# A decoder block on one core: weight sums with two transfers and two additions a unit, loaded one at a time, and the last unit's values added by VectorE

## The chip, the core and the metric

The kernel runs on one core of one Trainium2 chip. The metric is the device time of one execution in microseconds. The core has five instruction streams that matter here: TensorE (PE, matrix products into the PSUM banks), VectorE (DVE), ScalarE (ACT), GpSimd (POOL) and SyncE (SP). SyncE issues most transfers between the chip's memory (HBM) and the on-chip buffer (SBUF); GpSimd issues the transfers that add what they bring to what already lies at the destination (`accum_op=ALU.add`, called accumulating transfers below).

## What is computed

One decoder block over 16 meta tokens and 512 tokens of width 1024, in float32:

```python
h = layer_norm(concat([meta, x]), emb_ln_g, emb_ln_b)
proj = h @ w_in                                # 1024 x 10240, split in ten parts of 1024 columns
q_d, k_d, v_d, g_d, q_s, k_s, v_s, g_s, m_d, m_s = split(proj)
y_d = rms_norm(differential_attention(q_d, k_d, v_d)) * (1 - lam_init)   # 8 heads, softmax with ALiBi
y_s = stick_breaking_attention(q_s, k_s, v_s)                            # 16 heads of 64
br_d = (y_d * silu(g_d)) @ w_br_diff
br_s = (y_s * silu(g_s)) @ w_br_sb
merged = sigmoid(m_d + b_gate[0]) * br_d + sigmoid(m_s + b_gate[1]) * br_s
h = layer_norm(2 ** 0.25 * h + merged @ w_out, ln_g, ln_b)
return h[16:]
```

Every product of float32 values is made of three TensorE products of rounded parts: high x high, high x low and low x high.

## The kernel before

**Units.** The work is cut into 16 units (`UNITS`, line 70): eight differential heads ("d"), then eight pairs of stick-breaking heads ("s"). In unit u TensorE computes the scores and values of unit u, and among them, as filling, the key and value projections of unit u+1, the query projection of unit u+2 and some gates. `run` (line 571) takes the projections as generators and calls the other steps when an estimated time has come. After the units come the branch products ("BD", "BS"), the merge and the output product.

**Weights.** `items` (line 89) lists all operands in the order in which the products use them, each 128 x 512; `loads` lists what SyncE must bring for them. `prep(h)` (line 192) is called once a product and prepares the operand four products ahead: `hi` casts it on ScalarE into the rounded high part `wh` (line 183), `lo` subtracts on VectorE to get the low part `wl` (line 188), `add` makes a sum where the next operand is one, and `fetch` issues loads for which a buffer has come free. `wh` and `wl` have six buffers each. The loads have rings of their own: `raw` (six buffers) for plain tiles, `rawk` (five) for the sums of the key and value weights, `rawa` (four) for those of the branch weights.

**Seven products in place of eight.** From unit 5 on (`SEVEN`) the keys and values of a unit are computed together, with one 2 x 2 block scheme that needs seven products and sums of weight blocks (`stage_kv`, line 674, its products on line 693). With a11, a12 (halves of the key weights) and a21, a22 (halves of the value weights) the operands are, in this order: a11, a21+a11, a21+a22+a11, a12, a21+a22, a22, and a21+a22+a11+a12. Three `rawk` tiles a unit hold sums: a21 is loaded by SyncE, and GpSimd then issues one or two accumulating transfers on top (four a unit). The seventh operand is an addition on VectorE (line 169). The branch products use the same seven operands, but there the third is also an addition on VectorE, into a tile `sum`, so that two accumulating transfers do.

**When the sums are loaded.** `fetch` (line 134) goes through two lists, the `rawk` loads first, and issues as many as there are buffers free. `rawk` has no pool until unit 1 (line 958). A tile's accumulating transfers are written into the program three and six calls of `prep` after its load, through `placed` (line 222), which ties an instruction behind the one that stands ahead of it on its engine.

**What sets the order.** Ahead of the units and behind them the order of each engine is tied as written (`keep_order`). In the units only what goes through `placed` or `behind` is; the rest is ordered by the framework's scheduler, which may let an instruction go before others of its engine that are not ready yet. Each engine runs its instructions in the order that comes out.

**Keys.** The projected keys are cast into a staging tile `ks`, and SyncE copies them into the tiles `K[0]` and `K[1]` (lines 646 and 647), of which there is one set: the copy for unit u+1 waits for the scores of unit u (line 759), and the scores of unit u+1 wait for the copy.

**Biases.** GpSimd makes the slopes of each differential head by scaling the last head's tile (line 827, two buffers), at the start of each unit in program order.

**Values of the stick-breaking units.** `s_values` (line 918) gets each head's result in two halves of the 128 partitions. ScalarE copies one half across into `half` (line 933) and the other into `ys` (line 934), and GpSimd issues an accumulating transfer that adds `half` to `ys` (line 935). The gate (line 528) multiplies the result. In the last unit `ys` is a row of `ysT`, and behind its gate come the first splits for the branch products (`operands`, line 1030).

Of the kernel before, what the change touches and what calls it, by code (L numbers as in the profile page):

```python
# [9 lines left out]
F32 = mybir.dt.float32  # L10
# [3 lines left out]
ALU = mybir.AluOpType  # L14
PSUM = bass.MemoryType.PSUM

P = 128
# [18 lines left out]
ORDERED = [mybir.EngineType.PE, mybir.EngineType.DVE, mybir.EngineType.Activation, mybir.EngineType.Pool]  # L36
WARM = 14
SEVEN = 5
# [7 lines left out]
def hybrid_block_kernel(ctx: ExitStack, tc: tile.TileContext, x, meta, emb_g, emb_b, w_in, b_gate,  # L46
                        diff_lambda, subln_g, w_br_d, w_br_s, w_out, ln_g, ln_b, out):
    nc = tc.nc
    v, s, g, pe = nc.vector, nc.scalar, nc.gpsimd, nc.tensor
# [39 lines left out]
    items, names, loads = [], [], []  # L89
    for n, (kind, i) in enumerate(seq):  # L90
        if kind in ("BD", "BS", "wd", "ws"):
            if kind[0] == "B":
                tiles = [(w_br_d if kind == "BD" else w_br_s)[:, :, ts(2 * i + m, P)] for m in range(2)]
            else:
                tiles = [w_in[:, :, ds(COL[x + kind[1]] + i * P, P)] for x in "kv"]
            (a11, a12), (a21, a22) = [[w[:, ts(k, 4)] for k in range(2)] for w in tiles]
            ring = "rawa" if kind[0] == "B" else "rawk"
            o = len(loads)
            if ring == "rawa":
                loads += [(a11, None, "raw"), (a21, (a11,), ring), (a21, (a22,), ring), (a12, None, "raw"), (a22, None, "raw")]  # L100
                items += [o, o + 1, (o + 2, o), o + 3, o + 2, o + 4, (None, o + 3)]
            else:
                loads += [(a11, None, "raw"), (a21, (a11,), ring), (a21, (a22, a11), ring), (a12, None, "raw"),
                          (a21, (a22,), ring), (a22, None, "raw")]
                items += [o, o + 1, o + 2, o + 3, o + 4, o + 5, (o + 2, o + 3)]
        elif n < 4:
            items += [None, None]
        else:
            c = COL[kind] + i * P
            items += [len(loads), len(loads) + 1]  # L110
            loads += [(w_in[:, ts(k, 4), c:c + P], None, "raw") for k in range(2)]
        names += [(kind, i)] * (len(items) - len(names))
# [9 lines left out]
        left[l] = 1  # L122
    raw0 = ypool.tile([P, 4, KT, P], F32, tag="ys", name="raw0")
    raws, second, split, sums, later = {}, {}, [], {}, []
    rings = {"raw": (6, []), "rawk": (5, []), "rawa": (4, [])}
    sum_loads, other_loads = [[l for l, x in enumerate(loads) if (x[2] == "rawk") == y] for y in (True, False)]
    state = {"h": 0, "n": 0, "ahead": 4}
    pools = {"raw": wpool}
# [4 lines left out]

    def fetch(most=99):

        for order in (sum_loads, other_loads):
            while order and most:
                l = order[0]
                src, more, tag = loads[l]
                bufs, log = rings[tag]  # L140
                if len(log) >= bufs and left[log[-bufs]] or tag not in pools:
                    break
                raw = pools[tag].tile([P, 4, P], F32, tag=tag, name=tag, bufs=bufs)
                nc.sync.dma_start(raw if l < WOUT else raw.rearrange("p a b -> p (a b)"), src)
                if more is not None:
                    second[l] = [lambda raw=raw, x=x: g.dma_start(raw, x, accum_op=ALU.add) for x in more]  # L146
                    if tag == "rawa":
                        added(l)
                    else:
                        for n in range(len(more)):  # L150
                            later.append((state["n"] + 3 + 3 * n, lambda l=l: added(l)))
                        later.sort(key=lambda x: x[0])
                raws[l] = raw
                log.append(order.pop(0))
                most -= 1

    def added(l):

        if second.get(l):
            placed(second[l].pop(0), ORDERED[3:])  # L160

    def add(h):

        first, other = items[h]
        one = sums.pop(True) if first is None else raws[first]
        raw = one
        if first is not None and loads[first][2] == "rawa":
            raw = lp.tile([P, 4, P], F32, tag="sum", name="sum", bufs=1)
        v.tensor_tensor(raw, one, raws[other], op=ALU.add)
        for l in items[h]:  # L170
            if l is not None:
                left[l] -= 1
        sums[h] = sums[True] = raw

    def hi(h):

        assert len(split) == h
        item = items[h]
        assert not second.get(item)
        raw = raw0[:, h // 2, ts(h % 2, 4)] if item is None else sums.pop(h) if isinstance(item, tuple) else raws[item]  # L180
        wh, wl = [wpool.tile([P, 4, P], F32R, tag=w, name=w, bufs=6) for w in ("wh", "wl")]
        split.append((raw, wh, wl))
        s.copy(wh, raw)  # L183
# [38 lines left out]
    def placed(work, engines=ORDERED):  # L222

        ins = nc.cur_bb.bb.instructions
        n = len(ins)
        work()
        for e in engines:
            new = next((i for i in ins[n:] if i.engine == e), None)
            old = next((ins[m] for m in range(n - 1, max(n - 400, 0), -1) if ins[m].engine == e), None)
            if new is not None and old is not None:  # L230
                follow(new, old)
# [349 lines left out]


    with tc.tile_pool(name="att", bufs=1) as ap:
        apads = []
        for n in range(2):
            a = ap.tile([P, AW], F32, name=f"apad{n}")
# [331 lines left out]
        def s_values(unit, c, p, ta):  # L918
            V = unit["V"]
            v4, a4 = tails[c]  # L920
            own, oth = ((LO, HI), (HI, LO))[c]
            av = pav.tile([P, 512], F32, tag="av", name="av")
            pe.matmul(av, V[c][:, 0, :], ta[0][0], start=True, stop=False)
            pe.matmul(av[:, QOFF[4]:], v4, a4, start=False, stop=False)
            for j in range(1, 4):
                o = av[:, QOFF[j]:]
                pe.matmul(o, V[c][:, j, :], ta[j][0], start=False, stop=False)  # L927
                pe.matmul(o, V[c][:, j, :], ta[j][1], start=False, stop=False)
            pe.matmul(av, V[c][:, 0, :], ta[0][1], start=False, stop=True)
            if "y" not in unit:  # L930
                unit["y"] = gpool.tile([P, S], F32, tag="sg", name="ys")
            half = ap.tile([P, S], F32, tag="sq", name="half")
            s.copy(half[own], av[oth])
            s.copy(unit["y"][own], av[own])
            placed(lambda: g.dma_start(unit["y"][own], half[own], accum_op=ALU.add), ORDERED[3:])

# [18 lines left out]
        pending = []  # L955
        for u, (kind, n) in enumerate(UNITS):
            unit = units[u]
            if u + 4 == SEVEN:
                pools["rawk"] = ap
            last = u + 1 == len(UNITS)  # L960
            proj = [] if last else keys_values(units[u + 1], *UNITS[u + 1])
# [62 lines left out]
    first = len(nc.cur_bb.bb.instructions)  # L1024
    lp = ctx.enter_context(tc.tile_pool(name="late", bufs=1))
    lr = ctx.enter_context(tc.tile_pool(name="later", bufs=2))
    pools["rawa"] = lp
    LEFT, RIGHT = ts(0, 256), ts(1, 256)

    def operands(y):  # L1030
# [225 lines left out]
```

## Time and profile before

| what | before |
|---|---|
| median of three runs | 729.81 us (729.35 to 733.26) |
| profiled execution | 724.71 us |
| its span, first to last instruction | 722.9 us |
| granted TensorE clock | 0.996 |
| GpSimd's accumulating transfers for `rawk` | 44 of 256 KB, 6.0 us to landing |
| SyncE's loads for `rawk` | 33 of 256 KB, 4.1 us to landing |
| moved by DMA in all | 123.64 MB |

The profile is one execution. A row of the page's first part gives an engine's busy time, its share of the span and its instructions. A row of the table of stretches gives the stretch, its length, and then for PE, PEld (weight loads), DVE, ACT and POOL the busy time and the number of instructions, then the granted TensorE clock, the DMA share (mean busy share of 16 DMA engines; it can pass 1 where a transfer is counted whole) and GB/s. A row of the waits reads "who waited <- for whom: us in total, times, longest". A row of a timeline gives start, duration, engine (with "q" for an issue by an engine's sequencer), line, operation, output<-inputs, shape, count, and in brackets the idle time before it with what ended it. Times of TensorE's instructions overlap: a matmul's end is modelled, so the spacing of starts tells its rate.

### The profile page before, as it was taken

Reading aid. Unit: us, or ns where it says so; the run is one execution under the profiler, and the core shown is the slowest. Engines: PE = TensorE matmul, PEld = TensorE weight load, DVE = VectorE, ACT = ScalarE, POOL = GpSimd, SP = SyncE. Lnnn points to the kernel's source line nnn. Section 1 sums busy time; section 2 is a strip of 40 time slices with the busy share of each in tenths; the row PEclk is TensorE's granted clock in tenths of the full one; section 3 lists DMA queues with packets and bytes.
Section 4 is the critical chain, followed back from the end, with each engine's and each line's share of the span. In section 5 each row is a group of like instructions: output and inputs, shape, how many; then the busy total and the mean of one; then the engine's idle time right before and its main releaser. Section 6 shows DMA issues by size and latency. Waiting matters only on the chain.

```text
span 722.9 us, 13508 instructions
## 1 busy us (share of the span) xinstructions
PE 706.7 (98%) x4558; PEld 644.5 (89%) x4558; DVE 571.3 (79%) x1253; ACT 434.1 (60%) x1043; POOL 127.6 (18%) x153
## 2 busy tenths in 40 slices
PE   9998999999999999999999999999999999999994
PEld 8998999989999888989989899988878998999884
DVE  6886897887796767979887898976267888788887
ACT  5674776767576677867767586765356456555300
POOL 3251110122122120212132110000003202130002
PEclk9999999999999999999999999999999999999998
DMA  9398544778989795798897956556539837787902
GB/s 293 95 171 180 158 101 122 171 159 194 217 170 201 196 183 153 163 234 165 219 208 177 227 137 188 146 154 190 167 90 197 173 108 186 142 167 195 325 18 102
DMA packets 182343, 123.64 MB, mean 171 GB/s; under 512 B 9041, under 2 KB 165106, under 8 KB 182274
## 3 DMA queue, kind: packets, MB, share of 16 engines
q1 hardware_dynamic: 148130, 102.32, 49.0%
q0 software_dynamic: 33824, 19.40, 21.6%
q10 hardware_dynamic: 320, 1.06, 0.4%
q8 instruction: 36, 0.59, 0.3%
q14 instruction: 33, 0.27, 0.1%
HBM read 91.96 MB, written 9.44 MB: 140 GB/s over the span
## 4 chain that ended last, share of the span: by engine, by line
PE 79%; DMA 6%; DVE 6%; ACT 4%; issue 3%; POOL 1%; SPq 0%; ACTq 0%; DVEq 0%; POOLq 0%
PE q L693 15%; PE ps L496 10%; PE ps L497 10%; PE ps L498 10%; PE q L1063 8%; PE ps L512 7%; PE sc L759 5%; PE t L765 3%; DMA k<-ks 2%; PE t L770 1%; DMA lgb<-in_ln_b_dram 1%; DMA ss<-sm 1%; PE bank L387 1%; PE av L927 1%; ACT wh L183 1%
## 5 line engine op out<-in xcount | busy, mean ns | idle before, releaser
L188 DVE TENSOR_TENSOR wl<-raw,wh 128x512 fp32r<-128x512 f32 x169 | 114.8, 686 | 45.8 <-ACT wh L183 40.9
L496 PE MATMUL ps<-hTh,wh 128*128 128x512 f32 x368 | 144.6, 393 | 1.5 <-ACT wh L183 1.5
L497 PE MATMUL ps<-hTl,wh 128*128 128x512 f32 x368 | 144.7, 393 | 0.0
L498 PE MATMUL ps<-hTh,wl 128*128 128x512 f32 x368 | 144.6, 393 | 0.0
L183 ACT CAST wh<-raw 128x512 fp32r<-128x512 f32 x169 | 103.0, 620 | 35.3 <-PE ps L497 26.4
L496 PEld LDWEIGHTS ps<-hTh,wh 128*128 128x128 f32 x368 | 69.2, 188 | 15.2 <-ACT wh L183 1.9
L146 POOL DMA_DIRECT2D rawk<-in_w_in_dram x44 | 58.7, 1649 | 131.2 <-DMA rawk<-in_w_in_dram 49.5
L498 PEld LDWEIGHTS ps<-hTh,wl 128*128 128x128 f32 x368 | 69.1, 188 | 14.0 <-DVE wl L188 0.4
L497 PEld LDWEIGHTS ps<-hTl,wh 128*128 128x128 f32 x368 | 69.2, 188 | 13.1
L759 PE MATMUL sc<-k,A 128*128 128x264 f32 (+3 forms) x320 | 67.9, 300 | 3.3 <-DMA k<-ks 3.1
L1063 PE MATMUL q<-gh,wh 128*128 128x256 f32 x224 | 63.5, 283 | 0.3 <-ACT t L1072 0.3
L1063 PE MATMUL q<-gl,wh 128*128 128x256 f32 x224 | 63.4, 283 | 0.0
L1063 PE MATMUL q<-gh,wl 128*128 128x256 f32 x224 | 63.4, 283 | 0.0
L776 DVE TENSOR_TENSOR al<-t,ah 128x512 fp32r<-128x512 f32 (+2 forms) x88 | 45.6, 525 | 22.2 <-ACT ah L775 18.4
L913 DVE TENSOR_TENSOR_SCAN e<-e,diag 128x528 f32<-128x528 f32 (+1 forms) x64 | 53.8, 846 | 7.0 <-ACT e L907 7.0
L775 ACT CAST ah<-t 128x288 fp32r<-128x288 f32 (+3 forms) x88 | 39.9, 462 | 29.9 <-PE t L765 20.0
L759 PEld LDWEIGHTS sc<-k,A 128*128 128x128 f32 x320 | 50.5, 189 | 6.5 <-issue 3.4
L693 PE MATMUL q<-tS,wh 128*128 128x264 f32 x176 | 50.8, 290 | 0.0
L693 PE MATMUL q<-tl,wh 128*128 128x264 f32 x176 | 50.3, 286 | 0.0
L693 PE MATMUL q<-tS,wl 128*128 128x264 f32 x176 | 50.0, 285 | 0.0
L512 PE MATMUL ps<-hTh,wh 128*128 128x264 f32 x160 | 46.1, 288 | 0.0
L512 PE MATMUL ps<-hTh,wl 128*128 128x264 f32 x160 | 45.8, 287 | 0.0
(291 smaller groups left out, 1843.4 us busy)
## 6 DMA issues: line engine op xcount, KB each, us to landing
raw<-in_w_in_dram SPq DMA_DIRECT2D x141, 256.0 KB, 3.4
rawk<-in_w_in_dram POOLq DMA_DIRECT2D x44, 256.0 KB, 6.0
rawk<-in_w_in_dram SPq DMA_DIRECT2D x33, 256.0 KB, 4.1
k<-ks SPq DMA_DIRECT2D x60, 132.0 KB, 3.6
raw<-in_w_out_dram SPq DMA_DIRECT2D x16, 256.0 KB, 3.2
k<-ks SPq DMA_DIRECT2D x60, 66.0 KB, 3.4
A<-low SPq DMA_DIRECT2D x28, 128.0 KB, 3.3
raw<-in_w_br_diff_dram SPq DMA_DIRECT2D x12, 256.0 KB, 3.9
```

The source lines that it names most:

```text
L146: second[l] = [lambda raw=raw, x=x: g.dma_start(raw, x, accum_op=ALU.add) for x in more]
L183: s.copy(wh, raw)
L188: eng.tensor_tensor(wl, raw, wh.bitcast(F32), op=ALU.subtract)
L496: pe.matmul(ps, wh[:, k % 4, :], hTh[:, k, M:], start=(k == 0), stop=False)
L497: pe.matmul(ps, wh[:, k % 4, :], hTl[:, k, M:], start=False, stop=False)
L498: pe.matmul(ps, wl[:, k % 4, :], hTh[:, k, M:], start=False, stop=(k == KT - 1))
L512: pe.matmul(ps[:, :H2], a[:, k % 4, :], b[:, k, ts(c, H2)], start=(k == 0 and m == 0), stop=(k == KT - 1 and m == 2))
L693: pe.matmul(bank, a[:, k, :], b, start=start and k == 0 and j == 0, stop=k == 3 and j == 2, skip_group_check=not start)
L759: pe.matmul(ps[:, :n], q, K[:, m, k0:k0 + n], start=(m == 0), stop=(m == 1))
L776: v.tensor_tensor(l, t[:, o:o + w], h.bitcast(F32), op=ALU.subtract)
L913: v.tensor_tensor_scan(rev, rev, diag[0][:, L - nk:][:, ::-1], 0.0, ALU.mult, ALU.max)
L1063: pe.matmul(bank, a[:, k, :], b[:, n, k, :], start=start and k == 0 and m == 0, stop=k == 3 and m == 2, skip_group_check=not start)
```

## The change

The units' weight sums take the form that the branch sums have: five loads a unit in place of six, two accumulating transfers in place of four, and two additions by VectorE in place of one, the first into a tile `sum` (one buffer, in the units' pool). The `rawk` ring has four buffers in place of five. It opens in unit 2 in place of unit 1, and `fetch` issues at most one `rawk` load a call. A tile's transfer is written into the program three calls of `prep` after its load, or when the tile is asked for. Apart from that, in the last unit (p == 7) VectorE adds `av` and `half` into `ysT`; ScalarE's second copy and the accumulating transfer are gone there.

```diff
@@ -96,13 +96,8 @@
-            if ring == "rawa":
-                loads += [(a11, None, "raw"), (a21, (a11,), ring), (a21, (a22,), ring), (a12, None, "raw"), (a22, None, "raw")]
-                items += [o, o + 1, (o + 2, o), o + 3, o + 2, o + 4, (None, o + 3)]
-            else:
-                loads += [(a11, None, "raw"), (a21, (a11,), ring), (a21, (a22, a11), ring), (a12, None, "raw"),
-                          (a21, (a22,), ring), (a22, None, "raw")]
-                items += [o, o + 1, o + 2, o + 3, o + 4, o + 5, (o + 2, o + 3)]
+            loads += [(a11, None, "raw"), (a21, a11, ring), (a21, a22, ring), (a12, None, "raw"), (a22, None, "raw")]
+            items += [o, o + 1, (o + 2, o), o + 3, o + 2, o + 4, (None, o + 3)]
...
-    rings = {"raw": (6, []), "rawk": (5, []), "rawa": (4, [])}
+    rings = {"raw": (6, []), "rawk": (4, []), "rawa": (4, [])}
...
-        for order in (sum_loads, other_loads):
+        for order, most in ((sum_loads, 1), (other_loads, most)):
             while order and most:
...
-                    second[l] = [lambda raw=raw, x=x: g.dma_start(raw, x, accum_op=ALU.add) for x in more]
+                    second[l] = lambda raw=raw, more=more: g.dma_start(raw, more, accum_op=ALU.add)
                     if tag == "rawa":
                         added(l)
                     else:
-                        for n in range(len(more)):
-                            later.append((state["n"] + 3 + 3 * n, lambda l=l: added(l)))
+                        later.append((state["n"] + 3, lambda l=l: added(l)))
...
-        if second.get(l):
-            placed(second[l].pop(0), ORDERED[3:])
+        if l in second:
+            placed(second.pop(l), ORDERED[3:])
...
+        for l in items[h]:
+            added(l)
         one = sums.pop(True) if first is None else raws[first]
-        raw = one
-        if first is not None and loads[first][2] == "rawa":
-            raw = lp.tile([P, 4, P], F32, tag="sum", name="sum", bufs=1)
+        raw = one if first is None else pools["sum"].tile([P, 4, P], F32, tag="sum", name="sum", bufs=1)
         v.tensor_tensor(raw, one, raws[other], op=ALU.add)
...
+            if p == 7:
+                v.tensor_tensor(unit["y"][own], av[own], half[own], op=ALU.add)
+                return
             s.copy(unit["y"][own], av[own])
             placed(lambda: g.dma_start(unit["y"][own], half[own], accum_op=ALU.add), ORDERED[3:])
...
-            if u + 4 == SEVEN:
+            if u + 3 == SEVEN:
                 pools["rawk"] = ap
```

More of the change, by code (lines that the diff above doesn't have):

```diff
@@ L178, in hi @@
         item = items[h]
-        assert not second.get(item)
+        added(item)
         raw = raw0[:, h // 2, ts(h % 2, 4)] if item is None else sums.pop(h) if isinstance(item, tuple) else raws[item]
@@ L583, in hybrid_block_kernel @@
     with tc.tile_pool(name="att", bufs=1) as ap:
+        pools["sum"] = ap
         apads = []
@@ L1026, in hybrid_block_kernel @@
     lr = ctx.enter_context(tc.tile_pool(name="later", bufs=2))
-    pools["rawa"] = lp
+    pools["rawa"] = pools["sum"] = lp
     LEFT, RIGHT = ts(0, 256), ts(1, 256)
```

## The prediction

> **What bounds the kernel now.** I read the page's first part, then the table of 20 us stretches, then TensorE's own waits.
>
> ```profile
> span 722.9 us, 13508 instructions
> PE 706.7 (98%) x4558; PEld 644.5 (89%) x4558; DVE 571.3 (79%) x1253; ACT 434.1 (60%) x1043; POOL 127.6 (18%) x153
> ```
> ```profile
> 0.00:20.00 20.00, 18.34 (x120) 17.29 (x121) 13.88 (x33) 11.43 (x28) 6.17 (x23) 1.00 0.94 295
> ...
> 40.00:60.00 20.00, 20.00 (x144) 18.91 (x142) 17.92 (x55) 13.39 (x36) 10.26 (x10) 1.00 1.20 212
> 60.00:80.00 20.00, 17.77 (x142) 17.37 (x141) 14.73 (x44) 11.10 (x30) 0.00 (x0) 1.00 0.53 130
> ...
> 300.00:320.00 20.00, 19.12 (x114) 16.75 (x113) 15.70 (x30) 12.02 (x30) 6.06 (x5) 1.00 1.10 222
> ...
> 420.00:440.00 20.00, 20.00 (x135) 18.52 (x134) 19.83 (x39) 15.20 (x41) 2.16 (x2) 1.00 0.64 153
> ...
> 520.00:540.00 20.00, 18.48 (x82) 14.67 (x81) 10.41 (x19) 9.46 (x17) 0.81 (x1) 1.00 0.29 68
> ...
> 700.00:720.00 20.00, 13.74 (x84) 12.17 (x82) 17.58 (x30) 0.51 (x1) 5.22 (x9) 0.92 0.24 93
> ```
> ```profile
> PE sc L759 <- DMA k<-ks: 3.1, 2, 2.2
> PE ps L496 <- ACT wh L183: 1.5, 1, 1.5
> ...
> PE q L1063 <- ACT t L1072: 0.3, 1, 0.3
> ```
>
> TensorE is idle for 722.9 - 706.7 = 16.2 us. The stretches (second number: TensorE busy) say where: 1.7 at the start, 6.3 in 700 to 720 and the last 2.9 after it, when its work is over, and in between only 2.23 (60 to 80), 0.88 (300 to 320) and 1.52 us (520 to 540), beside under 0.8 in small pieces. The waits name these three: twice the scores wait for a key copy, once a projection waits for a weight cast. So the kernel is bound by TensorE's work, which the change leaves alone; it can win these 4.6 us (a little more where a restart is ragged) and lose whatever new wait it makes.
>
> **The change part by part.** *First stall (60 us).* In this order: the chain, SyncE's timeline, SyncE's waits in 48 to 62 us, GpSimd's timeline, the sum transfers issued in 38 to 60 and their landing times, then the landing times of the key copies of line 647 issued in 48 to 62, and of the same line in 62 to 140:
>
> ```profile
> 55.47 0.18 PE sc L759 x2
> ...
> 56.89 5.40 DMA k<-ks
> ```
> ```profile
> 31.06 2.78 SPq L144 DMA_DIRECT2D rawk<-in_w_in_dram  x5
> 39.68 8.78 SPq L144 DMA_DIRECT2D raw<-in_w_in_dram  x7
> ```
> ```profile
> SPq L646 <- DMA raw<-in_w_in_dram: 2.3, 2, 1.8
> ```
> ```profile
> 57.26 2.54 POOL L827 TENSOR_SCALAR bias<-bias 128x528 f32<-128x528 f32 x1
> ```
> ```profile
> L146 POOL DMA_DIRECT2D rawk<-in_w_in_dram x7: 1282/1830/3499, 38.5 to 56.5; - x7
> ...
> DMA to landing us min/median/max: 5.8/9.8/14.4
> ```
> ```profile
> DMA to landing us min/median/max: 5.1/7.7/10.6
> ```
> ```profile
> DMA to landing us min/median/max: 1.9/2.1/3.4
> ```
>
> The program asks for the five sum loads at the start of unit 1, but SyncE, idle, issues them at 31.06, and seven accumulating transfers (1+2+1+1+2 for the five tiles) run from 38.5 on, under unit 0. They take 9.8 us at the median, the DMA share is 1.20, and the copies of unit 1's keys take 7.7 instead of 2.1 us. They are also issued late: SyncE's queue holds line 646 for 2.3 us until older raw loads have landed. The copy issued at 56.89 lands at 62.29 and TensorE loses 2.23 us.
>
> After the change the ring opens a unit later, and each transfer is placed behind the GpSimd instruction ahead of it in program order, which is then the slope scaling of unit 2. That is the row at 57.26: it cannot come earlier, since its buffer is unit 0's. So in 38 to 57 no accumulating transfer runs at all, and four run from about 60. Without the burst the copies go out behind the last readers of unit 0's keys (the scores at 55.47), near 56, and at 1.9 to 3.4 us they land before TensorE runs out of other work, at 62.3 - 2.2 = about 60. Bounds: 0 to 2.4 us won (the wait and a slow restart); I take **2.2**, near the whole, because the wait ends on this copy alone. If SyncE again issues the plain loads at 31, they have landed before the keys are copied, as they do now.
>
> *Second stall (318 us) and the units from 5 on.* One chain row, GpSimd's timeline, and from the page the DMA issues:
>
> ```profile
> 312.74 5.94 DMA k<-ks
> ```
> ```profile
> 300.57 4.24 POOL L146 DMA_DIRECT2D rawk<-in_w_in_dram  x3
> 311.95 1.28 POOL L146 DMA_DIRECT2D rawk<-in_w_in_dram  x1 [7.14 <-DMA rawk<-in_w_in_dram]
> ```
> ```profile
> rawk<-in_w_in_dram POOLq DMA_DIRECT2D x44, 256.0 KB, 6.0
> rawk<-in_w_in_dram SPq DMA_DIRECT2D x33, 256.0 KB, 4.1
> ```
>
> The eleven units lose 11 of 33 loads and 22 of 44 transfers, 33 x 256 KB. Four transfers run here between 300 and 318, the DMA share is 1.10, and a key copy takes 5.94 us. With two transfers a unit the crowd is half as large, but the whole middle of the kernel is re-ordered when it is scheduled anew, so this stall may stay or a like one appear elsewhere. Bounds: from a loss of 0.9 to a gain of 1.0; I take **0.5**, the half of the traffic that goes. GpSimd's 22 issues (about 1.3 us each) save nothing by themselves: GpSimd is busy 18%.
>
> *Last unit's values.* Rows of the timeline, by engine:
>
> ```profile
> 525.49 0.81 POOL L935 DMA_DIRECT2D ysT<-half  x1 [11.21 <-ACT ysT L934]
> ```
> ```profile
> 524.01 0.58 ACT L933 COPY half<-av 64x512 f32<-64x512 f32 x1 [5.07 <-PE av L929]
> ...
> 528.82 0.93 ACT L1044 CAST gh<-ydT 128x256 fp32r<-128x256 f32 x2 [3.62 <-DMA ysT<-half]
> ...
> 532.74 1.12 ACT L183 CAST wh<-raw 128x512 fp32r<-128x512 f32 x2
> ```
> ```profile
> 528.76 0.69 DVE L528 TENSOR_TENSOR ysT<-sg,ysT 128x512 f32<-128x512 f32 x1 [9.47 <-DMA ysT<-half]
> ```
> ```profile
> 531.27 0.39 PE L497 MATMUL ps<-hTl,wh 128*128 128x512 f32 x1
> 531.49 0.39 PE L498 MATMUL ps<-hTh,wl 128*128 128x512 f32 x1
> 533.40 0.50 PE L496 MATMUL ps<-hTh,wh 128*128 128x512 f32 x1 [1.52 <-ACT wh L183]
> ```
>
> Both VectorE and ScalarE stand until the transfer lands at about 528.7; the casts of weights behind them come at 532.74, and TensorE, which starts a matmul every 0.22 us, starts one 1.91 us after the other. In the change VectorE adds as soon as `half` is there: 524.01 + 0.58 + about 0.65 (the neighbouring 128x512 row is 0.69, the 64x512 copy 0.58) = 525.3. That is 3.4 us sooner; the first weight cast would end near 529.9, ahead of 531.7. The stall needs only 1.91 - 0.22 = 1.7 us to go. Queued behind the new wait on VectorE are the gate of line 528 and the splits, which waited longer before; ScalarE loses the second copy. Bounds 1.5 (the wait's own row) and 1.7; I take **1.7**.
>
> *What is added.* One more addition in each of eleven units, and its cover:
>
> ```profile
> L169 DVE TENSOR_TENSOR rawk<-rawk,raw x11: 664/691/1114, 130.2 to 440.3; 128x512 f32<-128x512 f32 x11
> ```
> ```profile
> ACT wh L183 <- PE ps L497: 41.7, 38, 2.4
> ...
> ACT wh L183 <- PE q L693: 7.7, 12, 1.8
> ```
> ```profile
> 288.43 2.42 PE q L693 x20
> ```
>
> That is 11 x 0.69 = 7.6 us of VectorE. What hides it is the lead: casts run four products ahead, 48 matmuls of 0.12 us = 5.8 us at the least, and it is ScalarE that waits for TensorE to free a weight buffer (49 us in all), not the reverse. The branch products already run with an addition for the third and the seventh operand, and line 1063 lost 0.3 us in all. If the cover went, a unit would pay addition and cast, about 1.3 us. The addition also waits for the sum's transfer, with VectorE's softmax work queued behind it; but the ring of four runs two units ahead. The first operand's buffer is held for one product (1.45 us) more: nothing, by the same lead; up to 1.45 us a unit without it. I take **0** for all of this.
>
> Sum: 2.2 + 0.5 + 1.7 = 4.4 us. The profiled execution took 724.71 us (its span and 1.8 around it), the median of the runs is 729.81, 5.1 longer, which no row explains; I carry the 4.4 us over unchanged: **725.4 us**.
>
> A sentence apart: the Trainium skill, page "DMA: Bandwidth & Descriptors", section "Anatomy of one DMA — SWDGE (gpsimd) path", fits a transfer issued by GpSimd at about 2.0 us plus its bytes over 436 GB/s, so an estimate of 2.6 us for 256 KB and 4.2 us of data movement for all seven; by that they could not crowd the key copies out, the first two terms would be 0 and the sum 1.7. The trace's 5.8 to 14.4 us disagrees.
>
> **The rivals.** *R1, the burst only moves.* The four transfers run from 60 to about 72, beside unit 2's query copies and the raw loads, and a later copy becomes the late one. For it: rows at 38 to 57 show what a burst does. Against it: four transfers, not seven, and unit 2's keys are copied only from 76 on. It gives the first term back: 725.4 + 2.2 = **727.6**.
>
> *R2, the sums are not what delays the keys.* Seven raw loads of 256 KB (the row at 39.68) go out beside them; if they are the crowd, both key stalls stay: 729.81 - 1.7 = **728.1**. Against it: the copies of the next units, with raw loads but no burst, land in 2.1 us. By the Trainium skill's figure above it would go this way. That the change does not do what it says belongs here too: "one at a time" may be undone by the free order on SyncE, as the five loads at 31.06 show.
>
> *R3, the additions reach TensorE: slower.* In 420 to 440 VectorE is busy 19.83 of 20 us. If VectorE falls behind by more than the 5.8 us lead, each of eleven units pays 1.3 us, 14.3 in all: 725.4 + 14.3 = **739.7**. Against it: TensorE was full in that very stretch, and VectorE has 21% idle over the span.
>
> **How the numbers follow.** About 0.5% (3.65 us, hence 726.16) is what a measurement of this kernel can tell from no change. Forecast 0.60 (723.0 to 727.2, 0.53 of it beyond 0.5%), R1 0.16, R2 0.11, R3 0.06, and 0.07 for a re-ordering none of these names (0.03 faster, 0.04 no change). Faster 0.53 + 0.03 = 0.56; same 0.07 + 0.16 + 0.11 + 0.04 = 0.38; slower 0.06. The range: at best 2.4 + 1.0 + 1.7 = 5.1 us go, 724.7, less half the width of the three runs (729.35 to 733.26), some 2 us: 722.5; at worst the last term alone stays, 728.1, plus the same 2: 730. R3 is left out.
>
> **What would show it.** Right: TensorE's waits name no key copy near 60 and no weight cast near 530; GpSimd's first sum transfer starts after 57; line 647's copies in 48 to 62 land in some 2 to 4 us. R1: the 60 us wait is gone and one of like size stands between 60 and 100. R2: it stays though no transfer runs before it. R3: TensorE waits for the cast behind line 169 in the units. A stall of a new kind in the re-ordered units would make the sum wrong with every step right.

## The result, and the profile after

| | median us | lowest to highest | ratio to before, 95% interval |
|---|---|---|---|
| before, 13 executions | 728.64 | 724.82 to 733.26 | |
| changed, 13 executions | 721.62 | from 721.16 | 0.9911 [0.989, 0.9933] |
| changed, a second set of 12 | 722.13 | 721.07 to 725.38 | 0.9932 [0.9911, 0.9954] |

The change makes the kernel 7.0 us faster (728.64 - 721.62), where 4.4 were forecast; 721.62 lies below the range of 722.5 to 730. The profiled execution of the first set was a disturbed one (2058.82 us, TensorE at about a third of its rate), as was that of one experiment (the control among the idle products, of which only times are used), so the profile below is of the second set. It is that set's slowest execution: 725.38 us, span 723.6, clock 0.993.

The page's first part, changed kernel:

```profile
span 723.6 us, 13419 instructions
PE 707.0 (98%) x4558; PEld 646.1 (89%) x4558; DVE 577.4 (80%) x1266; ACT 433.3 (60%) x1041; POOL 98.1 (14%) x129
```

What TensorE waited for in it:

```profile
PE q L1061 <- ACT t L1066: 2.5, 1, 2.5
PE warm L302 <- POOL idents masks.py:199: 1.4, 1, 1.4
PE q L688 <- DVE kvt L708: 1.0, 1, 1.0
PE sc L754 <- POOL k L600: 0.2, 1, 0.2
```

The lines have moved up by a few: 759 is 754 here, 693 is 688, 1063 is 1061. The waits for a key copy and for a weight cast are gone. In their place stand one of 1.0 us in the first seven-product unit (near 261 us, until VectorE has read a result for `kvt` out of its PSUM bank) and one of 2.5 us among the branch products. GpSimd's timeline, and the landing times of the key copy of line 642 (647 before) issued in 48 to 62 us:

```profile
56.86 1.53 POOL L822 TENSOR_SCALAR bias<-bias 128x528 f32<-128x528 f32 x1 [18.47 <-DVE mn L837]
58.34 1.52 POOL L141 DMA_DIRECT2D rawk<-in_w_in_dram  x1
59.52 4.43 POOL L141 DMA_DIRECT2D rawk<-in_w_in_dram  x3
```
```profile
DMA to landing us min/median/max: 1.9/1.9/1.9
```

No sum transfer goes out before 58.34, and the copies that took 7.7 us at the median take 1.9. The timeline around the last unit's values:

```profile
521.84 0.69 DVE L930 TENSOR_TENSOR ysT<-av,half 64x512 f32<-64x512 f32 x1 [5.31 <-ACT half L928]
522.57 0.69 DVE L522 TENSOR_TENSOR ysT<-sg,ysT 128x512 f32<-128x512 f32 x1
...
526.42 1.13 ACT L177 CAST wh<-raw 128x512 fp32r<-128x512 f32 x2
```

The gate follows the addition at once, and the casts come with no stall behind them. These two steps went as the prediction said, and the wait near 318 us, of which it counted on half, is gone altogether. How far TensorE is ahead shows in the branch products, first before, then changed (count, duration, and the first and last start):

```profile
L1063 PE MATMUL q<-gh,wh x224: 278/283/384, 555.6 to 669.1; 128*128 128x256 f32 x112
```
```profile
L1061 PE MATMUL q<-gh,wh x224: 277/283/582, 550.9 to 667.9; 128*128 128x256 f32 x112
```

The first starts 4.7 us sooner, near the 4.4 of the sum; the last only 1.2 us sooner, and this execution's span is no shorter than before's (723.6 and 722.9). Two questions follow: why the median falls by more than the sum, and why this execution loses what it had won.

### The profile page after: what moved, and what is told of

The parts are those of the page before. It is cut to its first block, busy times and chain, and to the rows that moved or that the text cites. A ratio compares the mean times of both kernels' runs of the same rounds, so it can differ in the third digit from the quotient of the medians.

```text
span 2057.0 us, 13419 instructions
## 1 busy us (share of the span) xinstructions
PE 2047.2 (100%) x4558; PEld 1520.8 (74%) x4558; DVE 601.5 (29%) x1266; ACT 453.5 (22%) x1041; POOL 98.2 (5%) x129
## 3 DMA queue, kind: packets, MB, share of 16 engines
HBM read 83.31 MB, written 9.44 MB: 45 GB/s over the span
## 4 chain that ended last, share of the span: by engine, by line
PE 100%; DVE 0%; POOL 0%; issue 0%; POOLq 0%
PE q L688 16%; PE ps L491 12%; PE ps L490 12%; PE ps L492 12%; PE ps L506 10%; PE q L1061 10%; PE sc L754 6%; PE pso L1186 6%; PE t L760 4%; PE bank L381 3%; PE t L765 2%; PE tv L721 1%; PE av L922 1%; PE av L923 1%; PE warm L302 1%; PE bank L335 1%
## 5 line engine op out<-in xcount | busy, mean ns | idle before, releaser
L491 PE MATMUL ps<-hTl,wh 128*128 128x512 f32 x368 | 334.8, 910 | 0.0
L492 PE MATMUL ps<-hTh,wl 128*128 128x512 f32 x368 | 334.1, 908 | 0.0
L490 PE MATMUL ps<-hTh,wh 128*128 128x512 f32 x368 | 332.9, 905 | 0.0
L490 PEld LDWEIGHTS ps<-hTh,wh 128*128 128x128 f32 x368 | 139.6, 379 | 93.0 <-issue 92.7
L491 PEld LDWEIGHTS ps<-hTl,wh 128*128 128x128 f32 x368 | 139.1, 378 | 93.0 <-issue 91.5
L492 PEld LDWEIGHTS ps<-hTh,wl 128*128 128x128 f32 x368 | 137.4, 373 | 92.6 <-issue 90.7
L754 PE MATMUL sc<-k,A 128*128 128x264 f32 (+3 forms) x320 | 162.2, 631 | 0.0
L760 PE MATMUL t<-idents,apad 128*128 128x128 f32 x240 | 104.1, 588 | 0.0
L506 PE MATMUL ps<-hTl,wh 128*128 128x264 f32 x160 | 100.4, 627 | 0.0
L1061 PEld LDWEIGHTS q<-gh,wh 128*128 128x128 f32 x224 | 98.7, 440 | 0.7 <-issue 0.7
```

What stands on the lines that cost most here:

```text
L490: pe.matmul(ps, wh[:, k % 4, :], hTh[:, k, M:], start=(k == 0), stop=False)
L491: pe.matmul(ps, wh[:, k % 4, :], hTl[:, k, M:], start=False, stop=False)
L492: pe.matmul(ps, wl[:, k % 4, :], hTh[:, k, M:], start=False, stop=(k == KT - 1))
L506: pe.matmul(ps[:, :H2], a[:, k % 4, :], b[:, k, ts(c, H2)], start=(k == 0 and m == 0), stop=(k == KT - 1 and m == 2))
L754: pe.matmul(ps[:, :n], q, K[:, m, k0:k0 + n], start=(m == 0), stop=(m == 1))
L760: pe.transpose(t[:, o:o + P], a[:, AOFF[i] + j * P:AOFF[i] + (j + 1) * P], ident)
```

## The experiments

All compare with runs of before on the same chip; its medians were 727.07, 727.67, 727.30 and 726.98 us in four sets. Of the theories named in what was expected, two are left at the end: C, that a wait of TensorE also lowers its clock, and D, that loads issued near the end hold the end back.

### The parts alone, and before again

Before a second time (no edit), the last unit's addition alone, and the later opening of the ring alone:

```diff
+            if p == 7:
+                v.tensor_tensor(unit["y"][own], av[own], half[own], op=ALU.add)
+                return
```
```diff
-            if u + 4 == SEVEN:
+            if u + 3 == SEVEN:
```

The changed kernel:

> The changed kernel as it is, to have its profile in an undisturbed execution. Theory A (the prediction's three stalls): TensorE's waits name no key copy near 60 us and no weight cast near 530 us, its idle time falls by 4 to 5 us from 16.2, and the median ratio is near 0.994. Theory B (the kernel before loses more to late transfers in most of its executions than in the one profiled): this kernel's waits are the same as under A, its times lie close together (within 0.4%), and the ratio is near 0.991.

Before again:

> The kernel before once more, for a second profile and for the scatter of its times. Theory A: the waits of the first profile return with the same sizes (key copies 2.2 us near 60 and 0.9 us near 318, weight cast 1.5 us near 533), span 722 to 724 us. Theory B: the waits for key copies have other sizes or places, 3 to 9 us in all, and the span is longer by what they are longer. Ratio 1.000 under both.

The last unit alone:

> The kernel before with one edit: in the last unit VectorE adds the halves. Theory A: the weight cast's wait near 533 us (1.5 us) is gone and nothing else changes, 1.7 us less, ratio 0.9977. If the wait was only moved to the first branch splits: ratio 1.000.

The later opening alone:

> The kernel before with one edit: the ring of the sums opens in unit 2, not in unit 1; still four transfers a unit and all free buffers at once. Theory A: the first key copies are no longer late, 2.2 us less, ratio 0.997, unless the seven transfers hit unit 2's copies (rival R1: ratio 1.000 and a key wait between 60 and 100 us). Theory B: 3 to 5 us less at the median, ratio 0.993 to 0.996.

Measured: the changed kernel 722.13 us (above); before again 725.43, 0.9988 [0.9963, 1.0013]; the last unit alone 725.34, 0.9968 [0.9942, 0.9993]; the later opening alone 722.98, 0.9943 [0.9919, 0.9967]. Before again is 1.6 us under before (727.07) with the same program, and the last unit alone is no lower than that, so a difference of two medians under some 2 us says little here. The later opening, one constant, brings 4.1 of the 4.9 us that the changed kernel gains in this set (727.07 - 722.13). TensorE's waits with it:

```profile
PE ps L496 <- ACT wh L183: 1.5, 1, 1.5
...
PE sc L759 <- DMA k<-ks: 0.3, 1, 0.3
```

It removes the wait at 60 us (2.2) and most of that at 318 (0.9), without one transfer fewer. That is 2.8 us of waits, for about 4.1 us of time (727.07 - 722.98). What more can vary shows in the profile of before again, whose profiled execution took 728.55 us, 3.8 more than the one that the prediction used. In both the scores wait near 60 us. The stretches of 2 us, the first before (columns as in the tables of stretches; the clock is the number after the five engines):

```profile
60.00:62.00 2.00, 0.20 (x2) 0.00 (x0) 0.69 (x1) 0.75 (x2) 0.00 (x0) 1.00 1.35 225
62.00:64.00 2.00, 1.57 (x13) 1.60 (x14) 0.64 (x3) 0.00 (x0) 0.00 (x0) 1.00 1.03 278
64.00:66.00 2.00, 2.00 (x20) 2.00 (x19) 0.60 (x4) 1.52 (x4) 0.00 (x0) 1.00 1.05 284
```

and before again:

```profile
60.00:62.00 2.00, 0.18 (x1) 0.21 (x2) 0.69 (x1) 0.52 (x2) 0.00 (x0) 1.00 1.35 221
62.00:64.00 2.00, 2.00 (x11) 2.00 (x11) 0.56 (x3) 0.00 (x0) 0.00 (x0) 0.55 1.20 290
64.00:66.00 2.00, 2.00 (x13) 2.00 (x12) 0.47 (x3) 0.92 (x3) 0.00 (x0) 0.60 1.15 271
66.00:68.00 2.00, 2.00 (x19) 2.00 (x18) 1.47 (x5) 0.96 (x2) 0.00 (x0) 1.00 0.24 61
```

After like waits the granted clock stays at 1.00 in the one and falls to 0.55 and 0.60 in the other, where TensorE is "busy" and starts 11 and 13 products in place of 20. The loss is (0.45 + 0.40) x 2 = 1.7 us beyond the wait. The last unit alone keeps the wait, and in its profile the clock is 0.83 in 60 to 70, which is the same 1.7 us.

The fall is not all of the 3.8 us. Among the branch products before again waits as the changed kernel does:

```profile
PE q L1063 <- ACT t L1068: 1.9, 1, 1.9
...
PE q L1063 <- ACT t L1072: 0.7, 1, 0.7
```

That is 2.6 us where the prediction's profile has 0.3. The fall (1.7) and 2.3 more of branch waits, less 0.6 of key waits (2.5 in place of 3.1), make 3.4 of the 3.8. The execution that the prediction used had neither.

Such a fall lowers the mean clock of an execution by 1.7 / 727 = 0.0023. The executions of before in the four sets, by mean clock:

| mean clock | falls, by 0.0023 each | executions of before | median us |
|---|---|---|---|
| 0.995 and over | none | 28 | 725.48 |
| 0.993 to 0.994 | one | 54 | 727.03 |
| 0.991 to 0.992 | two | 20 | 729.26 |
| 0.990 and under | three | 9 | 731.27 |

The steps of 1.6 to 2.2 us are what falls of 1.7 would make. The number of falls is inferred from the mean; only profiled executions show where they lie. A straight line through mean clock and time accounts for 0.58 of the variance of these 111 times; branch waits without a fall, as above, are one thing that it leaves out. The mean also takes in the time behind TensorE's last product, where a low clock costs nothing (0.85 in 710 to 720 us of before's first profile). Of 24 executions of the changed kernel none is under 0.993, and 13 are at 0.995 and over, with a median of 721.62. The other 11 have 722.48, only 0.9 us more, so for that kernel the table's steps are not borne out.

### Is it the fall? Products in the gap, and the same products elsewhere

In before, 18 idle products of 128x128 in float32 are put ahead of the scores of unit 1, where TensorE waited, and as a control ahead of those of unit 3 (`u == 3` in the last line). They go into a bank that the scores then overwrite.

```diff
-                for m in range(2):
-                    pe.matmul(ps[:, :n], q, K[:, m, k0:k0 + n], start=(m == 0), stop=(m == 1))
+                for m in range(-state.pop("awake", 0), 2) if "awake" in state else range(2):
+                    pe.matmul(ps[:, :n], q, K[:, m, k0:k0 + n], start=(m == 0), stop=(m == 1)) if m >= 0 else pe.matmul(ps[:, :P], ident, ident, start=True, stop=True)
...
-            last = u + 1 == len(UNITS)
+            last = u + 1 == len(UNITS); state.update({"awake": 18} if u == 1 else {})
```

In the gap:

> The kernel before, with 18 idle products of 128x128 ahead of unit 1's first scores (into the bank that those scores then overwrite): TensorE has some 2.0 us more work there, about as long as its wait near 60 us. Theory C (a wait near 2 us lets the granted clock fall to half for 3.4 us, 1.7 us more, in most executions): the wait is under 0.5 us, the clock in 60 to 70 is 1.00, and the median falls by 1 to 2 us (ratio 0.997 to 0.999) although 2.0 us of work were added. Theory A (only the wait itself counts): the added work takes the wait's place, ratio 1.000, or 1.003 where the wait stays.

The control:

> The control to before_awake: the kernel before with the same 18 idle products, ahead of unit 3's first scores, where TensorE did not wait. Theory C (before_awake won because TensorE stayed awake in the wait near 60 us): 1.5 to 2.2 us more than the kernel before (ratio 1.002 to 1.003), the key wait near 60 us stays and its stretch shows a lowered clock in most executions. If before_awake won by re-ordering the units: this one is re-ordered too and is no slower than the kernel before.

The added work was mis-sized: each product is two records, 36 in all, about 0.11 us apart, so some 4 us. The profile with the products in the gap:

```profile
L759 PE MATMUL sc<-idents x36: 272/275/275, 60.1 to 65.0; 128*128 128x128 f32 x36
```
```profile
60.00:70.00 10.00, 10.00 (x89) 9.96 (x88) 4.38 (x15) 3.63 (x10) 0.00 (x0) 1.00 0.84 176
```

Measured: 726.05 us, 0.9977 [0.9955, 1.0], from 725.25 to 727.46 only, with the clock at 0.995 or 0.996 in 10 of 12 executions. The control: 730.73, 1.0042 [1.0018, 1.0065], so 3.75 us more (726.98 before), the full price of the work. The same work costs 3.75 us in one place and -1.25 in the other (726.05 - 727.30), and the two intervals do not meet. That before itself becomes faster is not shown, since the first interval reaches 1.0; it becomes no slower and less scattered. Of the 5.0 us between the two places, the wait filled (2.2) and the key wait at 318 us, which is not in this schedule either (0.9), are 3.1. The 1.9 left are about one fall, but no profile shows which waits the control kept, and this profile has a branch wait of 0.2 us only. So the times agree with a fall that costs real time; what shows it directly is the spacing of TensorE's starts above.

### The waits among the branch products

The 2.5 us of the changed kernel: ScalarE's cast of a merged tile waits for an accumulating transfer (`ss` += `td`), and TensorE for ScalarE. The two waits go together, in the kernel before as in the changed one. ScalarE's, first before, then before again, then changed:

```profile
ACT mh L1104 <- DMA ss<-td: 3.5, 1, 3.5
```
```profile
ACT mh L1104 <- DMA ss<-td: 6.3, 1, 6.3
```
```profile
ACT mh L1102 <- DMA ss<-td: 6.3, 1, 6.3
```

TensorE then waits for 0.3, 2.6 and 2.5 us. With the later opening, the early opening and the products in the gap ScalarE waits for 1.5 to 1.8 us and TensorE for 0.2. In the experiments here VectorE does four of these six merges, with the cast one product later, or (`wait = 6 if j < 2 else 4 if j < 6 else 1`) four later:

```diff
-        wait = 6 if j < 6 else 1
-        if j < 6:
+        wait = 6 if j < 2 else 1
+        if j < 2:
```

Before and changed, one product later:

> The kernel before, but branch rows 2 to 5 are merged by VectorE in place of a GpSimd transfer (rows 6 and 7 already are), so that ScalarE's cast of the merged row waits for no transfer near 650 us. Theory A (both kernels lose 0 to 3.4 us there, by chance, and the change itself is worth the 4.4 us forecast): TensorE loses nothing in 640 to 670, the median falls to about 724.5 (ratio 0.996 to 0.998), and the fourfold spread of its times shrinks from 8 us to under 5. Theory B (the kernel before loses to late key copies by varying amounts): the spread stays near 8 us and the median falls by under 1 us.

> The changed kernel with the same edit: rows 2 to 5 merged by VectorE. Theory A: median about 720.0, its times within 2 us, and 4.4 to 4.8 us (0.6 to 0.65%) under before_merge. Theory B: median 721 as without the edit, 6 us or more under before_merge. If VectorE has no room in 640 to 670, both are slower than without the edit.

Before and changed, four products later:

> The kernel before with rows 2 to 5 merged by VectorE and their cast placed four products later in place of one, so that ScalarE waits neither for a transfer nor for VectorE. Branch phase without a wait of TensorE over 0.5 us. Theory C: 1 to 3 us under the kernel before (724.5 to 726.5), since the waits near 60 and 530 us stay. If the branch phase cost the runs nothing: 727.5.

> The changed kernel with the same edit. Theory C: no wait of TensorE over 1.2 us is left, the clock is 1.00 up to 710 us, times within 1.5 us, 719.5 to 721 us; 4.5 to 6 us under before_merge4. If the end is set by the last loads and VectorE rather than by TensorE: 721 to 722, no faster than the changed kernel, with a longer stretch after TensorE's last product.

Measured, in this order: 728.71 us, 1.0016 [0.9998, 1.0034]; 722.86, 0.9942 [0.9921, 0.9963]; 730.10, 1.0036 [1.0011, 1.0061]; 723.10, 0.994 [0.9919, 0.9961]. None is faster than the kernel it was made from, and all four medians that the theories expected were missed. What fits is the alternative named with the second, that VectorE has no room there: in 640 to 650 us of the first profile it is busy for 9.62 of 10 us. A wait of TensorE among the branch products stays in all four profiles (its longest 1.5, 1.8, 1.0 and 1.3 us), so the edit does not do what it was made for, and the four say little of what that wait costs. With before, four products later, the key wait is longer (why, no run shows), and the profile shows two of the prediction's waits, each followed by a fall:

```profile
PE sc L759 <- DMA k<-ks: 3.5, 1, 3.5
PE ps L496 <- ACT wh L183: 1.5, 1, 1.5
```
```profile
60.00:70.00 10.00, 6.67 (x43) 6.71 (x44) 3.78 (x12) 2.60 (x6) 0.00 (x0) 0.83 0.80 170
530.00:540.00 10.00, 8.47 (x29) 6.23 (x28) 8.97 (x18) 6.86 (x12) 0.00 (x0) 0.83 0.28 79
```

None of its 12 executions reaches 0.995; all 12 of the changed kernel with the same edit do. Among the branch products, too, a wait can bring a fall: in the changed kernel's profile the clock is 0.81, 0.50 and 0.84 in three stretches of 2 us behind the 2.5 us wait, 1.7 us again:

```profile
658.00:660.00 2.00, 0.34 (x1) 0.34 (x2) 1.84 (x4) 1.61 (x4) 0.04 (x1) 0.81 0.83 170
660.00:662.00 2.00, 2.00 (x11) 2.00 (x11) 1.51 (x4) 1.76 (x4) 0.00 (x0) 0.50 0.60 202
662.00:664.00 2.00, 2.00 (x16) 2.00 (x16) 1.99 (x4) 2.00 (x6) 0.00 (x0) 0.84 0.78 212
```

The wait and the fall, less the 0.3 us that before waits there, make 3.9 us; 3.5 of the 4.7 were lost (4.7 - 1.2). Why the transfer lands late in one execution and not in another stays open.

Over all profiles, of eight waits of TensorE of 1.8 to 3.5 us six were followed by a fall, and of eleven of 1.3 to 1.6 us one (the wait at the start is left out). So the longer waits bring most of the falls, but 2.2 us once brought none and 1.5 us once did.

### Which part of the change removes what

The changed kernel without its last unit's edit (the three lines of the first diff above); the changed kernel with the early opening (four transfers in the old place, loaded together), whose diff follows; and before with the first two diffs above together, so the change without the new sums:

```diff
-        for order, most in ((sum_loads, 1), (other_loads, most)):
+        for order in (sum_loads, other_loads):
...
-            if u + 3 == SEVEN:
+            if u + 4 == SEVEN:
```

> The changed kernel without the edit of the last unit (ScalarE copies and GpSimd adds, as before). Theory A: the weight cast's wait of 1.5 us near 529 us returns, 1.7 to 2.0 us more than the changed kernel, about 723.5, ratio 0.9955 to the kernel before.

> The changed kernel, but the ring opens in unit 1 as before and all free buffers are loaded at once: the new sums and the last unit's edit without the later opening. Four transfers then run from 38 us in place of seven. Theory A (the length of the burst sets the wait): the key wait near 60 us shrinks from 2.2 to under 1 us, 720.5 to 722 us at the median. If any burst under unit 0's last scores does the harm: the wait is 2 us still, 724 us. If the later opening was worthless: equal to the changed kernel.

> The kernel before with the later opening and the last unit's addition, without the new sums (still four transfers a unit, five buffers). Theory A and C (these two edits are the gain, the sums give nothing): 721.5 to 722.5 us, as the changed kernel. If the sums carry a part of their own: 1 us or more above the changed kernel.

Measured: without the last unit's edit 725.50 us, 0.9972 [0.9953, 0.9992]; TensorE's wait returns (third number the longest):

```profile
PE ps L490 <- ACT wh L177: 1.3, 1, 1.3
```

That is 3.4 to 3.9 us above the changed kernel's two medians (722.13 and 721.62), twice what was expected; no row explains what goes beyond the wait.

Early opening: 721.93 us, 0.9925 [0.9901, 0.9949]. Its four transfers go out at 38.55, in the old place, and the wait stays away (the second view has TensorE's waits, the one at the start left out):

```profile
38.55 5.45 POOL L141 DMA_DIRECT2D rawk<-in_w_in_dram  x4
```
```profile
PE q L688 <- DVE kvt L708: 1.1, 1, 1.1
PE q L1061 <- ACT t L1070: 0.2, 1, 0.2
```

So it is enough either to move seven transfers or to leave four. With four the crowd itself is hardly smaller: they take 10.0 us to landing at the median (9.8 before), and the copies of line 642 5.1 (7.7). What is gone is most of the hold in SyncE's queue, where line 646 waited 2.3 us for raw loads and its counterpart here, line 641, waits 0.9. The copy for which TensorE waited before, and the same copy here, are issued at:

```profile
56.89 0.62 SPq L646 DMA_DIRECT2D k<-ks  x1
```
```profile
54.66 0.62 SPq L641 DMA_DIRECT2D k<-ks  x1
```

Without the new sums: 722.12 us, 0.9925 [0.9899, 0.9951], as fast as the whole change. There seven transfers run where none did before; the rows are of the sum transfers issued in 50 to 80 us, and of the stretch 60 to 80, in which TensorE is busy throughout:

```profile
L146 POOL DMA_DIRECT2D rawk<-in_w_in_dram x7: 1282/1832/3476, 58.7 to 72.2; - x7
...
DMA to landing us min/median/max: 4.9/7.7/9.9
```
```profile
60.00:80.00 20.00, 20.00 (x155) 19.43 (x154) 17.13 (x53) 13.60 (x38) 9.14 (x9) 1.00 1.12 189
```

The new sums even cost something. In each of the six profiles with them a product near 261 us waits 0.9 to 1.1 us for VectorE (the row of line 688), in none of the nine without. There the new addition stands in VectorE's queue, which from then on is full until the instruction waited for; the rows are of the changed kernel, and behind them is the first row of the branch products without the new sums:

```profile
257.05 0.69 DVE L163 TENSOR_TENSOR sum<-rawk,raw 128x512 f32<-128x512 f32 x1 [0.38 <-DMA raw<-in_w_in_dram]
...
261.82 0.39 DVE L708 TENSOR_TENSOR kvt<-kvt,q 128x264 f32<-128x264 f32 x1
```
```profile
L1066 PE MATMUL q<-gh,wh x224: 277/283/387, 550.0 to 665.8; 128*128 128x256 f32 x112
```

TensorE starts the branch products at 550.0 us there and at 550.9 in the changed kernel.

### The end

Before's chain of waits has a load of `ln_b` by ScalarE's queue, and behind it a load of `w_out` and its cast:

```profile
671.98 9.44 DMA lgb<-in_ln_b_dram
...
682.33 4.90 DMA raw<-in_w_out_dram
687.25 0.62 ACT wo1h L1124
```

The changed kernel's chain has the same:

```profile
670.51 11.04 DMA lgb<-in_ln_b_dram
...
682.47 4.81 DMA raw<-in_w_out_dram
...
687.30 0.62 ACT wo1h L1122
```

The cast comes no sooner (687.30 and 687.25), though TensorE is ahead. The load of `ln_b` is issued 1.5 us sooner but takes 11.04 us in place of 9.44. From then on the chain is mostly VectorE's until the end, so what TensorE gains in this execution is held up by loads. Experiment: issue the loads of `ln_g` and `ln_b` two row blocks later, in the changed kernel and in the one without the new sums.

```diff
-                    if t == 0 and c == 0:
+                    if t == 2 and c == 0:
                         nc.scalar.dma_start(lgb[0][:, :], ln_g[0].partition_broadcast(P))
                         nc.scalar.dma_start(lgb[1][:, :], ln_b[0].partition_broadcast(P))
```

> The changed kernel with ScalarE's two loads of the last norm's rows issued in the third output block in place of the first. Theory D (the end is set by these loads, which hold the output weights back, and by VectorE behind them, so that one to two us of what TensorE gained are lost in the last stretch): the stretch from TensorE's last product to the end falls from about 11 to 9 us, 720.0 to 720.8 at the median, 1 to 2 us under the changed kernel. If TensorE sets the end: 721.5 to 722.2 as before.

> The later opening and the last unit's addition on the kernel before, without the new sums, with the same later loads. Theory D, and the new sums cost about 1 us in the re-ordered units: 719.5 to 721 us at the median, the fastest executions under 719; equal to or under after_lgb. If the new sums are worth something that the waits near 650 us hid: over after_lgb by 1 us.

Measured: 720.36 us, 0.9921 [0.9889, 0.9953], and 719.39, 0.9889 [0.986, 0.9918]. The output products with high weights (line 1186) in the changed kernel, then with the later loads:

```profile
L1186 PE MATMUL pso<-wo1h,mh x40: 278/389/389, 690.2 to 711.9; 128*128 128x512 f32 x24, 128*128 128x256 f32 x16
```
```profile
L1186 PE MATMUL pso<-wo1h,mh x40: 277/389/389, 686.7 to 708.4; 128*128 128x512 f32 x24, 128*128 128x256 f32 x16
```

From the last start to the end of the span it takes 723.6 - 711.9 = 11.7 us in the one and 717.8 - 708.4 = 9.4 in the other; in before it is 722.9 - 713.2 = 9.7. The early opening, with no wait in the branch products, also has 11.7 (708.9 to 720.6). So 2.0 us of TensorE's gain were lost at the end of these two executions, and with the later loads none is: the last loads of `w_out` are issued at 674.95 in place of 682.47. The later opening alone loses nothing there either (710.0 to 719.7, so 9.7), with the `ln_b` load in its chain, so this loss does not come with every gain. In the medians, of different sets, the later loads bring 1.8 and 2.7 us; the intervals overlap, so the times alone do not show it. The last kernel has the lowest median of all (six executions), 7.6 us below before in its set.

## Why the prediction was wrong

The miss is 725.4 - 721.62 = 3.8 us. Of it 1.2 are the base: the forecast started from 729.81, the median of three, and 13 executions gave 728.64. The other 2.6 are the effect, 7.0 for 4.4. (The range's lower end, 724.7 less 2, would be 722.7 rather than 722.5; 721.62 lies under both.)

**First stall, 2.2: right in size, the cause in part.** The wait is gone and the copies land in 1.9 us. R1 is refuted where it was strongest: with seven transfers from 58.7 to 72.2 us no wait follows. R2 is refuted too: four in the old place in place of seven suffice, with the raw loads as they were. But then the copies still land late, and it is their earlier issue that saves the wait; the hold in SyncE's queue, which the prediction names second, is what the shorter burst takes away. R2's support in the Trainium skill's page "DMA: Bandwidth & Descriptors", section "Anatomy of one DMA — SWDGE (gpsimd) path", falls with it: by that page's fit 256 KB are an estimate of 2.6 us, and the 22 transfers that are left take 5.4 us to landing at the median.

**Second stall, 0.5: too small, and the reason wrong.** The wait is gone whole, 0.9. It shrinks to 0.3 or goes when only the opening moves, with all 44 transfers; half of the traffic was not needed for it.

**Last unit, 1.7: the wait right, the time unsettled.** The wait goes with the edit and returns without it (1.3 us in that profile). In time the edit alone is worth 1.7 us against before and nothing against before again, and leaving it out costs 3.4 to 3.9.

**Additions, 0: wrong by 1 us.** TensorE waits for no cast behind line 163, so R3 as it stands is refuted. But the lead of the casts does not cover everything that waits for VectorE: once, near 261 us, a product waits 1.0 us for it. And the new sums bring nothing to set against that: 722.12 without them and 722.13 with them, and 719.39 against 720.36 with the later loads. The terms as they came out, 2.2 + 0.9 + 1.7 - 1.0 = 3.8, still make nearly the sum.

**The step that failed: "I carry the 4.4 us over unchanged".** The profiled execution was one without a fall of the clock (0.996) and with 0.3 us of branch wait, and the 5.1 us by which the median stood above it were noted as unexplained and then taken as untouched. One other execution shows what they can hold: 1.7 us of a fall and 2.3 of branch waits. Part of this is falls behind the very waits that the change removes. Executions at 0.995 and over compare as 725.48 to 721.62, 3.9 us, near the sum; over all 111 of before and 24 changed executions it is 727.14 to 721.71, 5.4 us. The 1.5 us between are, as far as mean clocks tell, falls that went with the waits. What is left to 7.0, 1.6 us, is that before's first set lay above its later ones (728.64 and 727.14), which no run explains. Against the 111 executions the base of 729.81 was 2.7 us too high and the effect 1.0 too small, so the larger part of the miss is a base from three executions. A second omission worked the other way: the end was taken to follow TensorE, and in two profiles 2.0 us of what TensorE wins stay there.

A rule of the Trainium skill bears on the fall: the page "TensorE: Matmul & The Clock Gate", section "Part 1: The HAM clock gate (the "warmup" mystery)", has the clock halve after an idle window of about 3.4 us, and the windows run on freely and do not start anew with a kernel. The half clock agrees with the rows (0.55 and 0.60; 1.7 us lost at half speed are 3.4 us of it). The threshold does not: waits of 1.5 and 1.9 us brought a fall, and one of 2.2 us in another execution did not. Where a window happens to begin may decide it; no run here shows the windows.

## What to carry to other kernels

Before carrying a sum from a profiled execution to a median, compare its mean clock with that of the other executions, look at a second profile of the same kernel, and count for each wait of TensorE near 2 us a chance of a fall, here 1.7 us more. When TensorE gains, look in the chain of waits for a late load that does not move with it: the gain can stop there. And try the parts of a change alone: here one constant and three lines did as much as the whole.

## What was not expected of the hardware

- A wait of TensorE of 1.5 to 3.5 us is followed in some executions by a granted clock of about half (0.55 and 0.60 in two stretches of 2 us, 1.7 us lost), and in others by none, with the same program.
- Such falls go with the waits, as far as mean clocks tell: the mean clock is 0.995 or more in 9 of 12 executions with the later opening alone, in 10 of 12 with idle products in the gap and in 13 of 24 of the changed kernel, in before in 28 of 111.
- Work put into a wait need not cost its time: with some 4 us of idle products before was no slower, and its range over 12 executions was 2.2 us (725.25 to 727.46), where that of 34 of before in the same set was 10.6 (722.82 to 733.38).
- One wait for an accumulating transfer near 650 us took ScalarE 3.5 us in one execution and 6.3 in another of the same program, and TensorE lost 2.3 us more in the second.
